# GEGLU MLP: the first products of w_gate begin on 256 tokens while the next 256 are still being transposed

## The chip, the cores and the metric

One core of a Trainium2 chip. The metric is the device time of the whole kernel in microseconds, median of several executions. A profiled execution also gives its span, some 2 us shorter than the time. The engines are PE (TensorE, matrix products), ACT (ScalarE), DVE (VectorE), GpSimd and SP (SyncE, which issues the loads).

## The reference

```python
gate = x @ w_gate                     # x: 8192 x 1024, w_gate and w_up: 1024 x 4096
up = x @ w_up
gate = 0.5 * gate * (1 + tanh(sqrt(2 / pi) * (gate + 0.044715 * gate ** 3)))
return ((gate * up) @ w_down)         # w_down: 4096 x 1024
```

## The kernel before

The kernel works on 8 passes of 1024 tokens with fast matrix multiplication on fp16 operands (seven block products P1 to P7 in place of eight, at the price of sums and differences of blocks, which DVE makes). Only the opening of the first pass matters here. It computes the first pair of column blocks directly, because the operands are not there yet: x and the first 512 columns of both weights come in as fp32, in 16 loads of 512 KB on one queue, and are cast on chip.

```python
for kh in range(2):                       # two halves of the contraction
    for gp in range(2): x0_load(0, gp, kh)              # tokens 0..511
    for w in range(2):  load_first(w, kh, slice(0, 256))
    for gp in range(2): x0_load(1, gp, kh)              # tokens 512..1023
for kh in range(2):
    for w in range(2):  load_first(w, kh, slice(256, 512))
```

The first pair interleaves casts (ACT, DVE), PE transposes of x with a copy out of PSUM, the memory that PE writes to (ACT for one 256-token half, DVE for the other), and products:

```python
def halves(kh):                           # w_gate's cast on ACT, in two instructions
    for ks in (slice(0, 2), slice(2, 4)):
        cast_first(0, kh, c0, act, ks)

warm(7)                                   # dummy matmuls of 512 columns
x0_cast(0, 0, 0)
x0_cast(0, 1, 0)
x0_transpose(0, 0, 0, 4, act)
warm(2)
x0_transpose(0, 1, 0, 5, dve)
warm(3)
halves(0)
cast_first(1, 0, c0, dve)                 # w_up
product(0, 0, 0, 0)                       # four matmuls of 512 columns each
product(0, 0, 0, 1)
product(0, 0, 1, 0)
x0_cast(1, 0, 0)
x0_transpose(1, 0, 0, 6, act)
# ... products, transposes and casts of the other tokens and the second half ...
x0_cast(1, 0, 1)
x0_transpose(1, 0, 1, 7, act)
x0_cast(1, 1, 1)                          # the 12th of the 16 loads
product(0, 1, 1, 0)
product(0, 1, 1, 1)
x0_transpose(1, 1, 1, 7, dve)
# ...
cast_first(1, 1, c1, dve)                 # the 16th and last load
sum_x(1); sum_w(0, 1, 0); sum_w(0, 1, 1); sum_x(2)
outputs(1, 0); outputs(1, 1)
sum_x(3); sum_w(0, 1, 2); sum_w(0, 1, 3); sum_x(4)
```

The second pair then runs its 14 product groups (four matmuls of 512 columns each; each product once for w_gate and once for w_up) in the order P1, P1, P2, P2, P5, P6, P6, P5, P7, P7, P4, P4, P3, P3. P2 goes into a bank of PSUM that ACT first fills with a copy of P1; P5, P6, P7 and P4 need the sums that DVE makes in the last lines above.

## Time and profile before

| | before |
|---|---|
| time, median of the first 3 runs | 2254.71 us (2253.45 to 2254.88) |
| span of the profiled run | 2252.9 us |
| PE busy | 2245.2 us |
| first product / second pair / its P3 begin | 9.31 / 26.80 / 38.37 us |

"P3" is the mark that I use below for "the opening is over": from there PE of before waits for nothing until about 279 us (in one experiment, sums_before, this does not hold). Two places that the prediction does not print matter for the result. First, DVE's casts of the 11th and 12th loads, each begun when the load lands:

```profile
18.88 0.69 DVE L304 TENSOR_SCALAR h_a<-h_a 128x1024 f16<-128x1024 f32 x1 [0.66 <-DMA h_a<-in_x_dram]
20.34 0.69 DVE L304 TENSOR_SCALAR h_a<-h_a 128x1024 f16<-128x1024 f32 x1 [0.77 <-DMA h_a<-in_x_dram]
```

### The profile page before, as it was taken

The page shows a single profiled execution, that of the slowest core. Times are in us where ns is not written, and L with a number is a line of the kernel's source. Part 1 is how long each engine was busy: PE and PEld are TensorE (multiplying, and loading weights), DVE is VectorE, ACT ScalarE, POOL GpSimd, SP SyncE. Part 2 cuts the span into 40 slices and gives each one's busy share as a digit, 9 for nine tenths or more (in the row PEclk, how much of TensorE's full clock was granted, in tenths as well). Part 3 has the DMA queues.
Part 4 walks back from the last instruction along what each step waited for, and adds up shares of the span by engine and source line. Part 5 has one row for each costly group of instructions (what it writes and reads, how often), then busy time and mean ns, then how long its engine had stood idle before and what let it go on. Part 6 is the DMA issues. An engine that isn't in the chain of part 4 may idle for free.

```text
span 2252.9 us, 42769 instructions
## 1 busy us (share of the span) xinstructions
PE 2245.2 (100%) x16616; PEld 1624.1 (72%) x16616; DVE 1560.6 (69%) x2189; ACT 956.4 (42%) x1863; POOL 680.6 (30%) x825
## 2 busy tenths in 40 slices
PE   9999999999999999999999999999999999999999
PEld 4444444444444445888888888888888888888888
DVE  6666458883588755777776677666776667866674
ACT  4443135651355622666125550356404653055520
POOL 1332013330133200555014550255402543044520
PEclk9999999999999999999999999999999999999999
DMA  9898969989999999999998999989999889988876
GB/s 243 164 209 216 288 180 242 262 267 289 247 227 249 279 311 348 328 350 363 302 337 278 316 300 321 321 270 324 307 327 316 286 308 318 318 315 275 283 289 232
DMA packets 309133, 642.46 MB, mean 285 GB/s; under 512 B 79104, under 2 KB 185344, under 8 KB 288384
## 3 DMA queue, kind: packets, MB, share of 16 engines
q1 hardware_dynamic: 254144, 566.57, 73.5%
q0 software_dynamic: 54784, 73.14, 19.3%
q8 instruction: 130, 2.13, 0.4%
q14 instruction: 75, 0.61, 0.1%
HBM read 574.36 MB, written 138.41 MB: 316 GB/s over the span
## 4 chain that ended last, share of the span: by engine, by line
PE 87%; DMA 2%; SPq 1%; DVE 0%; issue 0%; DVEq 0%
PE ps L857 40%; PE ps L1108 20%; PE ps L635 17%; PE ps L1000 10%; DMA wd_quads<-x_sums 1%; SPq L255 0%; DMA ring<-wd_ops 0%; PE ps L1130 0%; DVE x_sums L278 0%; DVE h_a L932 0%; DVE tmp L1140 0%; SPq L496 0%; DVEq L278 0%; SPq L544 0%
## 5 line engine op out<-in xcount | busy, mean ns | idle before, releaser
L857 PEld LDWEIGHTS <-ring 128*128 128x128 f16 x8320 | 814.1, 98 | 94.4
L834 POOL TENSOR_TENSOR h_a<-tmp 128x256 f16<-128x256 f32 x640 | 469.2, 752 | 839.1 <-ACT tmp L822 831.9
L857 PE MATMUL ps<-x_sums,ring 128*128 128x256 f16 x5760 | 655.8, 273 | 0.0
L819 DVE TENSOR_TENSOR tmp<-tmp,ps 128x512 f32<-128x512 f32 x640 | 414.3, 683 | 148.2 <-PE ps L857 100.7
L635 PEld LDWEIGHTS <-ring 128*128 128x128 f16 x2632 | 257.4, 98 | 311.9 <-issue 1.1
L804 ACT COPY tmp<-ps 128x512 f32<-128x512 f32 x520 | 304.5, 586 | 236.7 <-PE ps L857 164.4
L635 PE MATMUL ps<-x_sums,ring 128*128 128x512 f16 x1504 | 340.1, 379 | 0.6 <-DVE x_sums L267 0.4
L822 ACT ACTIVATE tmp<-tmp 128x256 f32<-128x256 f32 x640 | 264.3, 418 | 172.6 <-DVE tmp L817 79.2
L857 PE MATMUL ps<-x_b,ring 128*128 128x256 f16 x2560 | 305.6, 273 | 0.0
L817 DVE TENSOR_TENSOR tmp<-ps,tmp 128x512 f32<-128x512 f32 x240 | 165.4, 689 | 145.2 <-ACT tmp L804 99.9
L635 PE MATMUL ps<-x_b,ring 128*128 128x512 f16 x1128 | 259.3, 379 | 0.1
L661 POOL TENSOR_TENSOR h_a<-tmp 128x512 f16<-128x512 f32 x94 | 145.5, 1548 | 372.9 <-ACT tmp L659 265.6
L1108 PEld LDWEIGHTS <-h_a 128*128 128x128 f16 x2208 | 216.0, 98 | 25.0
L1000 PE MATMUL ps<-ring,h_a 128*128 128x512 f16 x1024 | 222.3, 379 | 0.7 <-DMA ring<-wd_ops 0.7
L1108 PE MATMUL ps<-ring,h_a 128*128 128x256 f16 x1888 | 212.6, 273 | 0.0
L1000 PEld LDWEIGHTS <-h_a 128*128 128x128 f16 x1152 | 112.7, 98 | 136.8 <-DMA ring<-wd_ops 1.2
L654 DVE TENSOR_TENSOR tmp<-ps,tmp 128x512 f32<-128x512 f32 x188 | 127.2, 684 | 113.7 <-ACT tmp L646 112.2
L1238 ACT ACTIVATE tmp<-ps 128x512 f32<-128x512 f32 x60 | 35.3, 598 | 362.5 <-PE ps L1108 274.5
L1171 DVE SCALAR_TENSOR_TENSOR tmp<-ps,tmp 128x512 f32<-128x512 f32 x119 | 80.4, 690 | 95.0 <-PE ps L1108 64.1
L360 DVE TENSOR_TENSOR ring<-ring 128x1024 f16<-128x1024 f16 x188 | 137.6, 745 | 10.5 <-DMA ring<-in_w_up_dram 6.2
L646 ACT COPY tmp<-ps 128x512 f32<-128x512 f32 x188 | 109.8, 586 | 78.5 <-PE ps L635 78.5
L1108 PE MATMUL ps<-ring,x_sums 128*128 128x256 f16 x1120 | 126.3, 273 | 0.0
(105 smaller groups left out, 1538.0 us busy)
## 6 DMA issues: line engine op xcount, KB each, us to landing
ring<-w_ops SPq DMA_DIRECT2D x480, 512.0 KB, 4.8
ring<-wd_quads SPq DMA_DIRECT2D x110, 1024.0 KB, 7.1
ring<-wd_ops SPq DMA_DIRECT2D x35, 1024.0 KB, 7.9
w_ops<-h_s SPq DMA_DIRECT2D x128, 256.0 KB, 6.7
out_dram<-tmp SPq DMA_DIRECT2D x127, 256.0 KB, 6.3
ring<-in_w_gate_dram POOLq DMA_DIRECT2D x23, 1024.0 KB, 10.4
ring<-in_w_up_dram POOLq DMA_DIRECT2D x23, 1024.0 KB, 18.0
wd_quads<-x_sums SPq DMA_DIRECT2D x131, 128.0 KB, 6.6
```

The costliest lines, as they stand in the source:

```text
L360: nc.vector.tensor_tensor(o, a, b, op)
L635: nc.tensor.matmul(ps(b, w), lhs[:, k], rhs[:, k, :], start=(first and k == 0), stop=(k == KH - 1), skip_group_check=True,)
L654: nc.vector.tensor_tensor(o, ps("b", w), o, ADD)
L661: nc.gpsimd.tensor_tensor(hq[TO[n]][:, i, :], tmp[:, t[n, 1]], tmp[:, t[n, 0]], MUL)
L804: nc.scalar.copy(tmp[:, t[o[1]]], ps_all[:, bank[o[2]]])
L817: nc.vector.tensor_tensor(d, b, a, SUB)
L819: nc.vector.tensor_tensor(d, a, b, ADD if o[4] == "add" else SUB)
L822: nc.scalar.activation(d, d, GELU, scale=GSC)
L834: nc.gpsimd.tensor_tensor(h, tmp[:, t[o[1]], MQ : 2 * MQ], g, MUL)
L857: nc.tensor.matmul(ps_all[:, bank[c], w * MQ : (w + 1) * MQ], lhs[:, w, k], rhs[:, k], start=(first and w == 0 and k == 0), stop=(k == KH ...
L1000: nc.tensor.matmul(ps_all[:, bank[b, g]], lhs[:, j, g * P : (g + 1) * P], dc[:, n, :], start=(first and j == 0), stop=(j == NP - 1), skip_ ...
L1108: nc.tensor.matmul(ps_all[:, bank[c], m * MQ : (m + 1) * MQ], lhs[:, j, m * P : (m + 1) * P], rhs[:, j, :], start=(first and j == 0 and m ...
```

## The change

The intent: the first products wait until both 256-token halves of x are transposed and copied, though w_gate's cast and the lower half are there earlier. So the products are split into a lower and an upper half, the dummy matmuls that filled the wait go, and the casts are written ahead of the second transpose.

```diff
         x0_transpose(0, 0, 0, 4, act)
         warm(2)
+        halves(0)
         x0_transpose(0, 1, 0, 5, dve)
-        warm(3)
-        halves(0)
         cast_first(1, 0, c0, dve)
-        product(0, 0, 0, 0)
-        product(0, 0, 0, 1)
+        for c in (lo, hi):
+            for j in range(2):
+                product(0, 0, 0, j, c)
         product(0, 0, 1, 0)
```

## The prediction

> **What bounds the kernel now.** I read the page first: the engines' busy shares and the chain that ended last. They say that TensorE (PE) carries the span of 2252.9 us.
>
> ```profile
> PE 2245.2 (100%) x16616; PEld 1624.1 (72%) x16616; DVE 1560.6 (69%) x2189; ACT 956.4 (42%) x1863; POOL 680.6 (30%) x825
> ...
> PE 87%; DMA 2%; SPq 1%; DVE 0%; issue 0%; DVEq 0%
> ```
>
> PE is idle for only some 8 us in all, so the tempting reading is "whatever takes time off PE shortens the span". But the change touches one spot, the first 12 us, and there the question is which wait ends last after it. So I went to the timeline of PE over the first 45 us, then to those of ScalarE (ACT) and VectorE (DVE), then to the DMA view of the first 24 us. In the timelines the columns are start, duration of the merged group (both us), engine, line, operation; in brackets is the idle time before it and what ended it.
>
> ```profile
> 6.33 1.06 PE L1284 MATMUL ps<-h_s 128*128 128x512 f16 x2
> 7.18 1.06 PE L314 MATMUL ps<-identity,h_a 128*128 128x128 f16 x8
> 8.04 1.49 PE L1284 MATMUL ps<-h_s 128*128 128x512 f16 x3
> 9.31 2.81 PE L1263 MATMUL ps<-x_b,ring 128*128 128x512 f16 x12
> 11.96 0.61 PE L314 MATMUL ps<-identity,h_a 128*128 128x128 f16 x8
> ...
> 17.25 2.75 PE L1263 MATMUL ps<-x_b,ring 128*128 128x512 f16 x12 [0.65 <-ACT x_b L317]
> 19.83 0.61 PE L314 MATMUL ps<-identity,h_a 128*128 128x128 f16 x8
> ...
> 26.80 3.89 PE L635 MATMUL ps<-x_b,ring 128*128 128x512 f16 x16
> 30.53 1.03 PE L635 MATMUL ps<-x_sums,ring 128*128 128x512 f16 x4
> 31.95 2.75 PE L635 MATMUL ps<-x_sums,ring 128*128 128x512 f16 x12 [0.40 <-DVE x_sums L267]
> ```
>
> L1284 are dummy matmuls that keep PE busy, L314 transposes of x, L1263 the first pair's products, L635 those of the second pair. The change works on the rows at 8.04 and 9.31. The row at 31.95 shows PE waiting for a difference of x blocks that DVE makes, so I look at who holds DVE and ACT:
>
> ```profile
> 26.23 1.05 ACT L340 CAST ring<-h_a 128x1024 f16<-128x1024 f32 x1 [0.40 <-DMA h_a<-in_w_gate_dram]
> 27.18 1.08 ACT L1275 ACTIVATE tmp<-ps 128x512 f32<-128x512 f32 x2
> 28.15 1.15 ACT L651 COPY ps<-ps 128x512 f32<-128x512 f32 x2
> ```
>
> ```profile
> 27.61 0.69 DVE L340 CAST ring<-h_a 128x1024 f16<-128x1024 f32 x1 [2.99 <-DMA h_a<-in_w_up_dram]
> 28.22 1.22 DVE L267 TENSOR_TENSOR x_sums<-x_b,x_b 128x2048 f16<-128x2048 f16 x1
> 29.35 1.41 DVE L360 TENSOR_TENSOR ring<-ring 128x1024 f16<-128x1024 f16 x2
> 30.68 1.22 DVE L267 TENSOR_TENSOR x_sums<-x_b,x_sums 128x2048 f16<-128x2048 f16 x1
> ```
>
> Both engines sit idle until one of the last two transfers of the first weights lands, and from there each runs without a gap into the instruction that PE waits for. The transfers themselves are 16 loads of 512 KB, issued at the start on one queue and waiting for no compute. Their casts mark the landings: x at 4.75, 6.13, 10.44, 11.80, 18.88 and 20.34 us, weights at 17.52, 23.29, 24.79, 26.23 and 27.61 us: one about every 1.4 us. The DMA view of 0 to 24 us in 40 slices shows them at 340 to 400 GB/s throughout:
>
> ```profile
> GB/s 0 0 0 68 225 253 376 406 403 353 370 376 360 362 370 379 389 389 389 389 379 399 374 364 350 348 348 357 376 382 382 389 391 346 345 346 353 350 346 343
> ```
>
> So the opening is bound by loading 8.4 MB, not by PE: 16 x 1.4 us = 22.4 us on top of the first landing's 4.7 (the first included) gives about 26 to 27 us, and the last landing is at 27.6.
>
> **What the Trainium skill says.** "TensorE: Matmul & The Clock Gate", Part 1: PE runs at 1.2 GHz until an activity window of some 3.4 us was busy, then at 2.4 GHz; the windows run freely. The trace agrees: the dummy matmuls of 512 columns start 0.425 us apart, the first products after 9.4 us 0.216 us apart. (The page's granted clock reads 1.00 even before that, so I go by the spacing.) The same page, "Engine queue depths": ACT and DVE are strict FIFO. The trace agrees: the x difference at 28.22 had both inputs by 14.6 us, yet stood behind the cast at 27.61. "DMA: Bandwidth & Descriptors", section "Where 436 GB/s comes from": some 358 GB/s per core bind HBM to SBUF transfers; the trace has 340 to 400, so no reserve. "PSUM — Partial Sum Buffer", "The four PSUM rules", rule 2: the first matmul of a group clears the written bits of the whole bank, so a lower half that starts the group and an upper half that doesn't are correct; the kernel does this already in its later halves, and no time hangs on it.
>
> **The change, part by part.**
> 1. Three dummy matmuls go: 3 x 0.425 = 1.28 us of PE at the slow clock.
> 2. The casts of w_gate are written ahead of the second transpose. On ACT nothing lies between: its queue is copy (6.57), two casts (7.59, 1.14 together), before and after. DVE's queue (copy 8.28, cast of w_up 9.08) is the same too. By itself this moves nothing.
> 3. Eight products of 512 columns become sixteen of 256: the same 4096 columns, at most eight more fixed costs of a few ns. The first eight need only the lower 256 tokens (copied by 7.58) and the cast of w_gate, whose first half ends at 7.59 + 0.62 = 8.21 and whose second at 8.73. They no longer wait for the upper tokens' copy at 8.28 + 0.69 = 8.97.
>
> New course of PE. The transposes stream out by 8.04. First products at about 8.25, two x 0.213 (256 columns, slow) to 8.68, a short wait for the second cast, two to 9.20, one slow to 9.41, then, if the clock rises where it does now, eleven x 0.109 = 1.20 to 10.61. Four of 512 (w_up, cast by 9.77): 0.86, to 11.47. Before, the transposes there began at 11.96: **a lead of about 0.5 us**. It passes through the next transposes (x cast done at 11.13 and 12.49, needed at 11.47 and 12.78), through DVE's and ACT's copies that follow PE, and brings the products at 17.25 to about 16.75.
>
> Then the loads take it back. Those twelve products end at 16.75 + 2.59 = 19.34, but the next transposes need the x cast of 18.88, done at 19.57: the lead falls to 19.83 - 19.6 = **0.2 us**. With it the second pair's first group starts near 26.6 instead of 26.80. Its third product set goes into a bank that ACT must fill first (copy of 28.15, done about 28.75); ACT is held by the landing at 26.23: cast 1.05, two GELUs, copy, back to back. PE now reaches that point at 26.80 + 8 x 0.216 = 28.53 and the set starts at 28.80, so PE waits 0.27 us already; after the change 0.47 us. From 28.80 nothing differs, and at 31.95 the same holds a second time through DVE. **Sum at 28.80: 0.5 gained, 0.3 lost at 19.6, 0.2 lost at 28.8, net 0.0 us.**
>
> **The rivals.**
> (a) The gain reaches the end. For it: after 36.6 us PE waits almost nowhere (one wait of 0.7 us at 279), so 0.5 or even 1.28 us there would show in full: 2254.2 or 2253.4. Against it: two later releases at 26.23 and 27.61 that hang on transfers alone. Even this would be 0.06% at best.
> (b) The clock rises a window later. For it: with the dummies gone PE has small holes near 8.1 and 8.7, some 0.3 us in the window 6.0 to 9.4, and the window before it, busy for 2.67 of 3.42 us, didn't raise the clock. Against it: 90% busy should do, though I know no threshold. Cost: products between 9.4 and 12.8 at half speed, 1.7 us lost against a start about 1 us earlier with holes; PE about 1.2 us late at 12 us instead of 0.5 early. The slack behind eats most of that: PE would be 0.4 late at 31.95, and the waits for DVE at 34.89 and 36.6 leave less than 0.1 to 0.3. Time 2254.8 to 2255.0.
> (c) The finer products bring a new wait, on PE's weight loads: sixteen loads of 98 ns against matmuls of 109 ns. They fit, barely; the kernel's bulk runs such pairs at 181.7 us per 1664, 109 ns each, on the chain. No change of time.
>
> **Range and chances.** All courses end within 1.3 us of one another, less than 0.1%. What remains is the scatter of runs: 2253.45 to 2254.88 before, and a profiled run at 2254.75. I predict 2254.6 us, 8 in 10 between 2252.8 and 2256.4. Over 2% would be 45 us, more than the whole opening: 0.5% each for faster and slower, 99% within 2%.
>
> **What would show it.** Right: the first product near 8.25, three dummies missing; the transposes of 11.96 about 0.5 earlier; a new PE wait of about 0.2 us for the x cast near 19.3; the cast of w_gate still at about 26.2 and that of w_up at 27.6; a longer PE wait before 28.8; the products of 31.95, 34.89 and everything after at the same times within 0.1 us. Wrong: matmuls of 256 columns 0.213 apart after 9.5 us (rival b); the row of 31.95 earlier by 0.3 us or more (rival a); or transfers that land at other times, which nothing in the change should cause but which would move the end by as much.

## More of the kernel before

Second, the one later wait of PE, for weights of the down projection (start, duration, engine and line, and in brackets the idle time before it):

```profile
279.21 2.98 PE L1000 MATMUL ps<-ring,h_a 128*128 128x512 f16 x13 [0.67 <-DMA ring<-wd_ops]
```

## The result, and the profile after

| | before | after |
|---|---|---|
| time, median of 6 runs | 2254.43 us (2253.45 to 2254.88) | 2254.86 us (2254.07 to 2255.98) |
| span of the first profiled run | 2252.9 us | 2252.8 us |

The ratio is 1.0003, with a 95% interval of 0.999 to 1.0015: the same. (A ratio is the mean time of one kernel's fast runs over that of the other's of the same rounds, so not quite the ratio of the medians.)

The sum of the prediction came out, but not all of its way. The timeline of PE in the changed kernel:

```profile
5.51 0.62 PE L314 MATMUL ps<-identity,h_a 128*128 128x128 f16 x8 [0.81 <-DVE h_a L304]
...
8.47 3.08 PE L1263 MATMUL ps<-x_b,ring 128*128 128x256 f16 x20 [0.96 <-ACT ring L340]
11.39 0.62 PE L314 MATMUL ps<-identity,h_a 128*128 128x128 f16 x8
...
16.73 2.75 PE L1263 MATMUL ps<-x_b,ring 128*128 128x512 f16 x12 [0.65 <-ACT x_b L317]
19.87 0.62 PE L314 MATMUL ps<-identity,h_a 128*128 128x128 f16 x8 [0.39 <-DVE h_a L304]
...
22.75 0.62 PE L314 MATMUL ps<-identity,h_a 128*128 128x128 f16 x8 [0.54 <-DVE h_a L304]
...
27.55 3.62 PE L635 MATMUL ps<-x_b,ring 128*128 128x512 f16 x16
31.01 3.88 PE L635 MATMUL ps<-x_sums,ring 128*128 128x512 f16 x16
35.08 3.64 PE L635 MATMUL ps<-x_sums,ring 128*128 128x512 f16 x16 [0.19 <-DVE ring L360]
38.55 3.62 PE L635 MATMUL ps<-x_b,ring 128*128 128x512 f16 x16
```

The lead is there: the second transposes begin at 11.39 instead of 11.96, the twelve products at 16.73 instead of 17.25. At 19.87 PE waits 0.39 us for the x cast, as foreseen. But then, at 22.75, it waits 0.54 us again, where before it had no wait (22.00), and the second pair begins at 27.55: 0.75 us *later* than before. From there the slack of the opening hides it, and the rows at 35.08 and 38.55 stand 0.19 and 0.18 us later than before, as does the last cast, which tells how late the loads ended in this run. DVE's casts in the changed kernel show where the second wait comes from:

```profile
19.12 0.69 DVE L304 TENSOR_SCALAR h_a<-h_a 128x1024 f16<-128x1024 f32 x1 [0.69 <-DMA h_a<-in_x_dram]
22.00 0.69 DVE L304 TENSOR_SCALAR h_a<-h_a 128x1024 f16<-128x1024 f32 x1 [2.19 <-DMA h_a<-in_x_dram]
...
27.79 0.69 DVE L340 CAST ring<-h_a 128x1024 f16<-128x1024 f32 x1 [2.42 <-DMA h_a<-in_w_up_dram]
```

The 12th load landed at 22.0 us instead of 20.3; the last one only 0.18 us later than before. Nothing in the change touches a load: the lists of instructions of ACT, DVE, GpSimd and SP are the same in both kernels. So the experiments had to settle three things: what swallows a lead or a lag of PE in the opening, whether the late load belongs to the change, and what moves the end of the span.

### The profile page after: what moved, and what is told of

It reads as the page before. It is cut to its first block, busy times and chain, and to the rows that moved or that the text cites. A ratio compares the mean times of both kernels' runs of the same rounds, so it can differ in the third digit from the quotient of the medians.

```text
span 2252.8 us, 42779 instructions
## 1 busy us (share of the span) xinstructions
PE 2243.4 (100%) x16621; PEld 1623.1 (72%) x16621; DVE 1562.7 (69%) x2189; ACT 955.4 (42%) x1863; POOL 680.8 (30%) x825
## 4 chain that ended last, share of the span: by engine, by line
PE 98%; DMA 1%; SPq 1%; DVE 0%; issue 0%; DVEq 0%
PE ps L857 40%; PE ps L635 25%; PE ps L1108 20%; PE ps L1000 13%; DMA h_a<-in_w_up_dram 0%; SPq L334 0%; DMA ring<-wd_ops 0%; SPq L298 0%; PE ps L1130 0%; DVE x_sums L267 0%; DVE ring L360 0%; DVE h_a L1276 0%; DVE ring L340 0%; DVE tmp L1140 0%; DVEq L1276 0%
## 6 DMA issues: line engine op xcount, KB each, us to landing
ring<-in_w_gate_dram POOLq DMA_DIRECT2D x23, 1024.0 KB, 10.8
```

## The experiments

One part of the change needed no chip. Before with only the casts moved ahead of the transpose gives, on all five engines, the same list of instructions as before: that part by itself does nothing.

The table has the reading of all 14 traces; the runs are told below it. "P3" and the second pair are PE's, "12th load" is the x cast that waits for it (a dash where DVE came to it later than it landed), "wait" is PE's wait at about 279 us.

| kernel | second pair | 12th load | P3 | wait | span |
|---|---|---|---|---|---|
| before | 26.80 | 20.34 | 38.37 | 0.67 | 2252.9 |
| before_again | 27.03 | 20.43 | 38.35 | 0.65 | 2252.8 |
| after | 27.55 | 22.00 | 38.55 | 0.41 | 2252.8 |
| after_again | 27.21 | 21.66 | 38.25 | none | 2251.9 |
| late2 | 29.18 | - | 39.54 | none | 2253.2 |
| late4 | 30.55 | - | 40.91 | 1.95 | 2256.8 |
| half_loads_before | 27.52 | left out | 37.88 | 1.46 | 2253.1 |
| half_loads_after | 26.41 | left out | 36.77 | none | 2250.3 |
| after_warm3 | 27.34 | 21.79 | 38.36 | none | 2252.0 |
| no_dummies | 28.63 | - | 38.99 | 0.71 | 2253.5 |
| sums_before | 26.86 | 20.38 | 37.42 | none | 2251.7 |
| sums_after | 27.42 | 21.87 | 37.78 | 0.88 | 2252.8 |
| cold_after | 28.31 | 20.27 | 38.67 | 1.79 | 2254.3 |
| fetch16 | 27.93 | 21.61 | 38.29 | 0.35 | 2252.5 |

One sum runs through the table: span minus P3 minus wait is 2213.5 to 2214.3 us in every row (before: 2252.9 - 38.37 - 0.67 = 2213.9; late4: 2256.8 - 40.91 - 1.95 = 2213.9; the 2214.3 is sums_before, where PE loses 0.65 us more between P3 and 43 us, told below). So a span is the opening, plus the wait at 279, plus a constant. And the wait is no buffer that swallows a lag: it was none in late2, whose PE was 1.2 us late, and 1.95 us in late4, whose PE was 2.5 us late. It scatters from run to run by more than the whole effect of the change, which is why the time of a single run says nothing here and the opening is read from the traces.

**The two kernels once more (before_again, after_again).** No edit.

> The kernel before, unchanged, for a second trace: what varies by itself from run to run. My theory: the moment at which the PE clock rises varies (9.4 us in the first trace of before, 5.5 us in that of the changed kernel, though no instruction before 8 us differs between them), the landings of the first loads vary by 0.1 to 0.5 us and the span by up to 1 us, while the two rejoin points stay tied to the landings: the second pair's last x difference group begins 7.3 us after the start of the last w_up cast (34.89 - 27.61). Rival: the earlier rise of the clock belongs to the change; then it is at 9.4 us here again.

> The changed kernel, unchanged, for a second trace. My theory: the first product begins some 0.1 us after the first w_gate cast, about 8.3 to 8.5 us; the second transposes at 11.4 to 11.5; the x transfer that landed only at 22.0 us in the first trace of it (20.34 in before) was scatter and is back near 20.4; the group after the waits for DVE begins 7.3 us after the last w_up cast. Rival: the late transfer belongs to the change, and it lands at 22 again.

PE's start and DVE's late cast in after_again:

```profile
8.39 3.51 PE L1263 MATMUL ps<-x_b,ring 128*128 128x256 f16 x20
...
34.78 3.64 PE L635 MATMUL ps<-x_sums,ring 128*128 128x512 f16 x16 [0.19 <-DVE ring L360]
```

```profile
21.66 0.69 DVE L304 TENSOR_SCALAR h_a<-h_a 128x1024 f16<-128x1024 f32 x1 [1.96 <-DMA h_a<-in_x_dram]
```

The early rise of the clock in the first trace of the changed kernel (eight transposes in 0.62 us at 5.51) was scatter: here they took 1.03 us. The group behind the waits for DVE began 7.28 us after the start of the last w_up cast in both (27.60 and 34.88, 27.50 and 34.78), as expected. But the late 12th load was not scatter: 21.66 in the changed kernel, 20.43 in before. That expectation missed, and its rival held.

**PE delayed on purpose (late2, late4).**

```diff
         cast_first(1, 0, c0, dve)
+        for _ in range(2):              # 4 in late4
+            product(0, 0, 0, 0)         # restarts its sum: the result stays right
         product(0, 0, 0, 0)
```

> Before with PE delayed on purpose: the first product group is computed two more times (each restarts its sum, the result stays right), 8 x 0.216 = 1.73 us (more if the clock is still slow). My theory, that the opening ends with the loads: a good part of the 1.73 is absorbed in the waits at 28.8, 31.95 and 34.89, leaving PE about 0.56 us later at 36.6; and the wait of 0.67 us for the weights at 279 absorbs the rest, so the span moves by less than 0.3 us. Rival, that PE time in the opening counts in full: 1.7 us later at 36.6 and at the end.

> As the last one with four repeats, 3.45 us. My theory: about 2.3 us late at 36.6, then 2.3 - 0.67 = 1.6 us late at the end if the transfer at 279 does not follow PE, 2.3 if it does. Rival: 3.45 us at both.

```profile
29.18 3.62 PE L635 MATMUL ps<-x_b,ring 128*128 128x512 f16 x16
32.63 7.07 PE L635 MATMUL ps<-x_sums,ring 128*128 128x512 f16 x32
39.54 3.62 PE L635 MATMUL ps<-x_b,ring 128*128 128x512 f16 x16
```

In late2 the second pair begins 2.38 us late (more than 1.73: the clock was slow for longer in this run), and P3 1.17 us late: 1.21 us are swallowed. In late4 it is 3.75 us and 2.54 us: again 1.21. The working in the expectation had 1.73 - 0.56 = 1.17. So the opening of before holds 1.2 us of slack for PE, and what goes beyond it counts in full. The second part of the expectation fell: the wait at 279 took nothing off reliably, as told above.

**Half of the loads left out (half_loads_before, half_loads_after).** Their outputs are wrong, which doesn't matter for the times.

```diff
-    for kh in range(2):
+    for kh in range(1):                  # loads of the first half only
         for gp in range(2):
             x0_load(0, gp, kh)
 ...
-            x0_piece(x0_f16, 2 * mh + gp, kh), x0_piece(x0_f32[mh], gp, kh), XSC, None, MUL
+            x0_piece(x0_f16, 2 * mh + gp, kh), x0_piece(x0_f32[mh], gp, 0), XSC, None, MUL
 ...
-        copy(o[:, ks], staging0(w, kh)[:, ks, cols])
+        copy(o[:, ks], staging0(w, 0)[:, ks, cols])
```

> Before without the loads of the second half of the contraction (8 of 16 transfers; the casts read the first half instead, so the result is wrong on purpose; the instructions of PE are the same, those of ACT and DVE the same in number and kind up to one). If the opening ends with its loads, PE's waits at 28.8, 31.95 and 34.89 go and the first matmuls of the group that begins at 38.37 in before begin 1.1 to 1.2 us earlier, at about 37.2. Rival, that the engines' own chains (DVE's sums) bound it and not the loads: 38.3 again.

> The changed kernel with the same loads left out. If the loads were what took the lead back, it now passes: the group of 38.37 begins about 0.5 us earlier than in half_loads_before, near 36.7. Rival: the lead is lost on PE or DVE itself; then both kernels begin it at the same time within 0.1 us. At the end of the span the wait for weights near 279 us (0 to 0.7 us in the six traces so far, 1.95 in one) may hide it either way.

P3 in half_loads_before, then in half_loads_after:

```profile
37.88 3.62 PE L635 MATMUL ps<-x_b,ring 128*128 128x512 f16 x16
```

```profile
36.77 3.62 PE L635 MATMUL ps<-x_b,ring 128*128 128x512 f16 x16
```

With the loads out of the way PE waits for nothing between its twelve products and 279 us, and the lead passes undiminished: the second transposes began at 12.68 and 11.51, 1.17 us apart, and P3 lies 1.11 us apart. (The lead is larger than 0.5 because the clock rose late in half_loads_before: its first twelve products took 3.43 us, not 2.81. That also is why P3 came at 37.88 and not at the expected 37.2: 0.72 us late already at 12.68, which stood at 11.96 in before.) So it is the loads that take the lead back in the real kernel. (Leaving them out also takes away the late pieces told of below, so these two runs do not tell the one from the other.)

**Slack taken out of the real kernel (sums_before, sums_after).** Two of DVE's sums stand behind the cast that waits for the last load, though their inputs are long there. Moved ahead:

```diff
+        sum_x(1)
+        sum_x(2)
         cast_first(1, 1, c1, dve)
-        sum_x(1)
         sum_w(0, 1, 0)
         sum_w(0, 1, 1)
-        sum_x(2)
```

> Before with the first two x differences on DVE moved ahead of the cast that waits for the last transfer (DVE stands idle for 3 us there, and both have their inputs). This takes 2.4 us out of DVE's chain behind the last landing. Expected: no PE wait at 31.95 and 34.89 any more, the group of 38.37 begins about 0.9 us earlier, 37.4 to 37.6 (the wait at 28.8, which ACT sets, stays). The span, at most 0.9 us shorter, 2252 to 2253, if the wait near 279 us does not take it; not to be told from 1.000 by the timed runs. Rival: the chain behind the last landing is not DVE's, and nothing moves.

> The changed kernel with the same move. If its fetch of instructions delays the x transfer as before, PE reaches the second pair at 27.2 to 27.5 and, with no wait left to hide that in, the group of 38.37 begins at 37.6 to 37.9: later than in sums_before by 0.2 to 0.4 us. So the change would cost a little where the slack is gone. If the lead of the prediction held, it would begin at the same time as in sums_before, 37.4 to 37.6. Ratio of the timed runs 1.000 within its interval.

P3 and what follows it in sums_before, then in sums_after:

```profile
37.42 3.62 PE L635 MATMUL ps<-x_b,ring 128*128 128x512 f16 x16
41.17 1.02 PE L635 MATMUL ps<-x_sums,ring 128*128 128x512 f16 x4
42.38 4.49 PE L635 MATMUL ps<-x_sums,ring 128*128 128x512 f16 x20 [0.18 <-DVE ring L360]
46.70 1.03 PE L635 MATMUL ps<-x_b,ring 128*128 128x512 f16 x4
```

```profile
37.78 3.62 PE L635 MATMUL ps<-x_b,ring 128*128 128x512 f16 x16
41.23 5.34 PE L635 MATMUL ps<-x_sums,ring 128*128 128x512 f16 x24
46.41 1.03 PE L635 MATMUL ps<-x_b,ring 128*128 128x512 f16 x4
```

Both expectations held up to P3 (the span of sums_before, 2251.7, lies just under its range). PE's waits for DVE's sums before P3 are gone and P3 comes 0.95 us earlier than in before. At P3 the changed order is 0.36 us *later*, because the 12th load lands late (21.87 against 20.38). But P3 is not the end of the opening here. Behind it sums_before loses 0.30 us before the row at 41.17 and 0.35 us before the one at 42.38, sums_after neither (the trace names no releaser for the first hole). DVE's next sum, which waits for a load of the following weights, shows why the second hole stands in one and not in the other:

```profile
39.83 0.69 DVE L360 TENSOR_TENSOR ring<-ring 128x1024 f16<-128x1024 f16 x1 [2.62 <-DMA ring<-in_w_up_dram]
```

```profile
39.41 0.72 DVE L360 TENSOR_TENSOR ring<-ring 128x1024 f16<-128x1024 f16 x1 [1.84 <-DMA ring<-in_w_up_dram]
```

It begins 0.42 us later in sums_before (39.83, against 39.16 to 39.57 in before, after, their repeats and after_warm3), and DVE runs from it without a gap into the sum that the row at 42.38 waits for. So at the same point of the program, 47.00 us in before and 47.18 in the changed kernel, sums_before stands at 46.70 and sums_after at 46.41: of the 0.95 us, 0.30 are left, and the changed order is now 0.29 us *ahead*. Whether that load came late by scatter is not shown (one trace of each), so these two runs do not show what the change is worth once the slack is gone, in either direction. The timed runs, 5 each: 2253.74 us for sums_before and 2254.18 for sums_after against 2254.17 for before, each with a ratio of 0.9998 (0.9985 to 1.001 and to 1.0012). Up to P3 the trace of sums_before has the shortest opening of all correct kernels, but neither 0.95 nor 0.30 us is to be told from nothing in the time.

**Fewer dummies (no_dummies, cold_after).** Before without the three dummies; the changed kernel without any.

```diff
-        warm(3)                          # no_dummies: from before
```

```diff
-        warm(7)                          # cold_after: from the changed kernel
 ...
-        warm(2)
```

> Before without the three dummies alone: the products still wait for the upper tokens' copy (DVE, 8.28 + 0.69 = 8.97). Expected: first product at about 9.05 instead of 9.31, second transposes about 0.25 us earlier than 11.96; fetch of instructions 3 matmuls later than in before less that lead, so about 20.2, and the x cast at 20.3 to 20.5; no change after 28.8 us. If the late x transfer came with the missing dummies, it lands near 21.7 here.

> The changed kernel with none of the dummy matmuls at all (9 fewer): PE's first work is the transposes at about 5.5 us. [...] Rival (b) of the prediction put PE about 1.2 us late in the second case and the end within 0.1 to 0.3 us. Expected: products at 0.213 us per 256 columns up to the rise; the group of 38.37 between 38.2 and 38.7. If the clock stays low longer than that, it is later by half of the extra time.

The first products of no_dummies:

```profile
9.12 4.84 PE L1263 MATMUL ps<-x_b,ring 128*128 128x512 f16 x12 [0.78 <-DVE x_b L317]
```

Only the start (9.12) came as expected. The twelve products took 4.84 us instead of 2.81: the clock stayed low until about 13.3 us (4.68 us to the next transposes, of which 12 x 0.216 = 2.59 would be all fast, leave 2.09 us, or ten matmuls with 0.211 extra). The second pair was 1.83 us late and P3 0.62: once more 1.21 us swallowed. In cold_after the clock also rose only near 13.3 us (16 x 0.213 + 4 x 0.427 = 5.12 us all slow, and the next transposes came after 5.18), later than I had expected (9 to 12.3 us, in a sentence cut above because it worked from the skill's window without naming it; its "second case" is the later end), and P3 at 38.67 is within the expected range. This is the prediction's rival (b), in a worse form than it assumed. Whether the missing dummies brought it about stays open: in the other twelve traces, six of them without the three dummies, the clock rose between 5.5 and 10.8 us.

**What makes the 12th load late (after_warm3, fetch16).** The DMA view has one fetch of instructions, 16 KB, in the opening. In half a microsecond of before (19.5 to 20.0) and of the changed kernel (18.5 to 19.0); the columns are queue, kind, packets, MB and the share of 16 engines' time:

```profile
q8 instruction: 1, 0.02, 14.1%
```

```profile
q8 instruction: 1, 0.02, 14.0%
```

The share is over 1/16 = 6.25% because the packet took longer (1.12 us) than the window. Each load is split over 16 DMA engines. In the changed kernel 15 of the 16 pieces of the 12th load had landed by 20.4 us and the last at 22.0; the same was so for every later load, down to the last. In before this begins with the 13th load (21.7 and 23.3). It looks as if one engine had fallen behind by about 1.4 us and never caught up (the trace does not number the engines; that it is the same one is read from the one late piece of each load). Over the runs with all loads, fetch16 apart, from first fetch to last:

| fetch stands at | kernels | first load with a late piece |
|---|---|---|
| 18.7 to 19.3 | after, sums_after, after_again, after_warm3 | 12th |
| 19.8 to 20.0 | before, sums_before, before_again | 13th |
| 21.4 to 22.5 | cold_after, late2, no_dummies, late4 | 14th |

In all of them PE was at, or at the end of, the same twelve products (17.25 in before) when the fetch came. So the likely reading is that PE's lead moved the fetch forward, ahead of the last pieces of the 12th load. Two kernels were to test this by moving the fetch through the count of PE's instructions.

```diff
-        warm(7)
+        warm(3)                          # after_warm3
```

```diff
         warm(7)
+        for _ in range(16):              # fetch16
+            nc.tensor.matmul(ps_all[:, 0, 0:64], warm_w, warm_x[:, 0:64], start=True, stop=True)
```

> The changed kernel with 3 instead of 7 dummy matmuls at the very start: PE comes 4 matmuls (8 rows) later to any point of its program. In both traces of the changed kernel the x transfer used at 20.34 us in before lands at 21.7 to 22.0, and one 16 KB fetch of instructions stands at about 18.7 to 19.2 us on one DMA engine, at 19.8 to 20.1 in both traces of before. Theory: the lead of PE brought the fetch forward, ahead of the last piece of that transfer. Then here the fetch is some 0.9 us later, the x cast is back at 20.3 to 20.5, and the second pair begins at 26.6 to 26.9 instead of 27.2 to 27.55. Rival, that the late transfer has another cause: it lands at 21.7 to 22.0 again.

> The changed kernel with 16 more dummy matmuls of 64 columns at its start, in PE's idle time before the first transposes (about 0.85 us at the slow clock). In eleven traces the 16 KB fetch of instructions came when PE had issued some 104 to 109 matmuls, and the first transfer due to land more than 0.6 to 1.1 us after its start, with all after it, was 1.4 us late. With 16 more PE would reach that count among the transposes at 15.0 to 16.2 us. Expected if the fetch is the cause: it stands at 15.6 to 16.4 us; the w_up cast of 17.6 goes at about 19.0, the x casts of 19.0 and of 20.35 at 20.3 to 20.5 and 21.7 to 21.9; the last w_up cast stays at 27.4 to 27.7; PE's second pair begins near 28 us and the group of 38.37 at 38.4 to 38.9. Rival, that the late x transfer of the changed kernel is another effect of PE's lead: w_up at 17.6 and x at 19.0 as in the changed kernel, and only the last x late.

Both missed on the fetch itself. In after_warm3 it came at 19.3, not 20, since PE ran a little ahead in this run (second transposes at 11.37), and the 12th load was late as in the changed kernel: no test. In fetch16 it came at 18.4, not 16. Something else happened there:

```profile
10.44 0.69 DVE L340 CAST ring<-x_sums 128x1024 f16<-128x1024 f32 x1 [2.16 <-DMA x_sums<-in_w_up_dram]
...
21.61 0.69 DVE L304 TENSOR_SCALAR h_a<-h_a 128x1024 f16<-128x1024 f32 x1 [0.72 <-DMA h_a<-in_x_dram]
27.44 0.69 DVE L340 CAST ring<-h_a 128x1024 f16<-128x1024 f32 x1 [1.69 <-DMA h_a<-in_w_up_dram]
```

One engine fell behind by 1.3 us already with the fourth load (10.44; 9.1 to 9.8 in the others), with no fetch in the record near it, and a second one from the 12th load on, with the fetch at 18.4. The loads came about as late as I had expected, and the last at 27.44, but not for the reason that I gave. The count on which I had based this (the fetch after 104 to 109 matmuls) was careless too: read again over all traces it lies between 92 and 116. So what is shown is this: the 12th load is late in all four traces of the changed kernel's order with a fetch at 18.7 to 19.3 us and in none of the seven with a later fetch, and in these eleven the fetch stands just before the first late piece. One of the seven, cold_after, has the changed order too: with PE late its 12th load was on time (20.27), so the order alone does not make it late. That the fetch *causes* it is the likely reading, not a proved one. fetch16 speaks for the fetch and against PE's lead itself, since PE was behind there (its twelve products at 17.88, against 17.25 in before) and yet a further late piece begins with the 12th load, but it is one run, disturbed already. What held the engine at the fourth load in fetch16 stays open.

## Why the prediction was right

- **"So the opening is bound by loading 8.4 MB, not by PE"**: right. Lag is swallowed up to 1.2 us (late2, late4, no_dummies: 1.21 each), and without half of the loads the lead passes whole (1.17 in, 1.11 out). Its sum was looser than it looks: the 16 landings have 15 steps, and SP issues the loads one after another from 0.7 to 18.7 us, not all at the start. What the prediction did not see is that the end hangs on one piece: in before, 15 of the 16 pieces of the last load had landed by 26.1 us and the last at 27.6. Nor is "no reserve" shown: the 358 GB/s taken from the skill is no ceiling here, since slices of the prediction's own row reach 406, and the measurement decides.
- **The parts of the change**: right. The moved casts alone give the same program. The first products began at 8.47 and 8.39 for a predicted 8.25; w_gate's cast began at 7.80 and 7.72, not at 7.59. The lead at the second transposes, predicted 0.5, was 0.57 in the first traces (with the clock up early) and 12.20 - 11.74 = 0.46 in the second.
- **"Then the loads take it back"**: right in kind (the transposes come at 19.87 and 19.75, later than PE would have reached them), but what was left of the lead was not 0.2 in either pair: 19.83 - 19.87, so none, in the first traces, where the 11th load's cast began at 19.12 and not at 18.88, and 20.06 - 19.75 = 0.31 in the second.
- **"the lead falls to 19.83 - 19.6 = 0.2 us. With it the second pair's first group starts near 26.6"**: this step failed. It started at 27.55 and 27.21. The step took the landing times of before as given, and the prediction said that nothing in the change should move them; but the 12th load landed 1.2 to 1.7 us later. In place of a lead of 0.2 us there was a lag of 0.2 to 0.75 us, and instead of a longer wait at 28.8 PE had none there.
- **"From 28.80 nothing differs"**: false for that time, true from 34.9 on. The group at 34.89 began 7.28 us after the last cast in before and 7.29 and 7.28 in the two traces of the changed kernel. The lag fitted into the 1.2 us of slack, so P3 came 0.18 us later in one pair of traces and 0.10 earlier in the other. The prediction was right on the time because the slack is wide, not because its lead was where it said: on this step it was lucky.
- **Rival (a), that the gain reaches the end**: no: P3 came 0.18 us later and 0.10 earlier in the two pairs. With the slack taken out the changed order is 0.36 us behind at P3 and 0.29 ahead at 46 us (sums_after against sums_before), so what it is worth there stays open.
- **Rival (b), the clock**: it did not decide the changed kernel (up by 5.5 us in one trace, during the first products in the other), but its size was set too low. PE can be 1.83 us late by it and 0.62 us of that counts, against 0.1 to 0.3. Its guess that 90% busy should do is shown by no run.
- **Rival (c), the finer products**: no sign of it. With the clock up, the twenty products from 8.47 to 11.39 took 2.92 us: 16 x 0.109 + 4 x 0.216 = 2.61, and the rest is the wait for the second half of w_gate's cast, which the prediction had.
- **The range**: the scatter of 2253.45 to 2255.98 us over both kernels has a part that the prediction named only in passing: PE's wait near 279 us, which went from none to 1.95 us over 14 traces.

## What to carry to other kernels

Before an opening is tuned, ask of each stage which transfer lands last and how much slack stands between that landing and the engine that you speed up: here 1.2 us, more than the change could win or lose. If you take slack out, read the gain behind the next landing and not only at your mark: two sums moved ahead of a waiting cast gave 0.95 us at P3, and 0.30 of it was left at 47 us, where PE had met a load of the following weights; the cost of the finer interleaving, 0.36 us at P3, had by then turned into 0.29 us ahead. And do not take landing times as given: an engine that runs earlier issued no load, yet a load landed 1.4 us later.

## What the Trainium skill lacked or had wrong

- "TensorE: Matmul & The Clock Gate", Part 1, says that the clock rises after a window of some 3.4 us of sustained work and that the moment varies by about 500 ns, more in places. Over these traces it rose between 5.5 and 10.8 us in twelve and near 13.3 us in two, with PE at work from 5.5 us (with holes of 0.35 to 0.8 us in those two). The spread, several us, is the thing to plan for.
- "Runtime: NRT & Kernel Launch", section "Instruction fetch mechanics", has the refill of instructions in 16 KiB blocks by a DMA queue and calls its cost mostly hidden. No page has that such a fetch occupies one of the 16 DMA engines for 1.1 us (1.12 to 1.16 in the opening of the eleven traces above), nor that a piece of each later load of a busy queue can then stay some 1.4 us late while the other 15 are on time (after: 20.4 and 22.0); that the fetch causes this is not proved. "DMA: Bandwidth & Descriptors" speaks of the split over the engines and of engines 7 and 15 being slower, not of this.
